# First layer's second and third modulation thirds: computed beside the attention with stationary weights, not beside the input projection

## The chip, the cores and the metric

The kernel runs as one program on one core of one Trainium2 chip. A core has a matmul engine (TensorE, PE in the rows; its loads of stationary operands are PEld), a vector engine (DVE), a scalar engine (ACT), a general engine (GpSimd, POOL) and a sync engine (SP) that issues the DMAs; each takes its instructions in the order in which they are written into the program, and they wait for one another by semaphores. The metric is the device time of one execution, in microseconds (us), lower is better.

## The reference, cut to what matters

Two layers of a transformer-like block over 256 context tokens and 1024 latent tokens, 1024 features, all in float32. Each layer draws six modulation vectors of 1024 features, for the latent tokens from `c` and for the context tokens from `c_ctx`:

```python
mod_x = (jax.nn.silu(c) @ ada_w[l] + ada_b[l])[:, None, :]          # 1024 x 6144 weights
mod_c = (jax.nn.silu(c_ctx) @ ada_w[l] + ada_b[l])[None, None, :]
sh1x, sc1x, g1x, sh2x, sc2x, g2x = jnp.split(mod_x, 6, axis=-1)     # the same for mod_c
hx = modulate(rmsnorm(xx, norm_mix_g[l]), sh1x, sc1x)               # first third: sh1, sc1
px = hx @ w_in[l]                          # columns of three mixers: GLA, attention, RWKV
mix_x = concatenate([oa_x, ob_x, oc_x]) @ w_out[l]
xx = xx + g1x * mix_x                                               # second third: g1, sh2
hx = modulate(rmsnorm(xx, norm_ffn_g[l]), sh2x, sc2x)               # third third: sc2, g2
xx = xx + g2x * swiglu(hx, ffn_w_gate[l], ffn_w_up[l], ffn_w_down[l])
```

So the first third (columns 0 to 2047) is needed before the layer's input projection, the other two (columns 2048 to 6143) only from the output projection on.

## The kernel before, in words

Features lie on the 128 partitions, tokens along the free dimension in groups of 256, 512 and 512. A dense product is made of three float32r matmuls (leading by leading, leading by trailing, trailing by leading parts), with a 128x128 weight tile stationary and up to 512 tokens moving. Weights come by DMA as `w_raw` (512 KB) and are split into two parts on ACT and DVE (`weight`, `split`, L343 and L344).

One layer runs through these stages, which are told by the names of the tiles that TensorE writes:

- the columns of RWKV of the input projection (`in_rwkv`, banks `ps_in`) with what is elementwise in them: a convolution over three tokens, decays, scans; much of that is on DVE. Results go to DRAM (`d_ab` among them);
- RWKV itself (`ps_g`, `ps_y`, `ps_w`, `ps_r`, `ps_s`) beside the other columns of the input projection, whose matmuls fill the time between (`mixers`). The first `ps_g` is its start;
- the attention (`swa_mixer`): scores `ps_ss`, softmax on DVE and ACT, transposes `ps_st` (L164), values `ps_so`, and the factors `ps_rb`; ten blocks of 128 queries in the first layer, two of them context blocks that see two tiles of keys, the others up to five. The states of GLA from the right (`ps_gu`) run beside it. Transposes, `ps_rt` and `ps_rb` share three PSUM banks (tag `t`);
- the output projection (`ps_o`, `out_first`) beside the rest of GLA (`ps_ga`, `ps_go`), the norm, the feed-forward part (`ps_gu` of `w_gate` and `w_up`, `ps_d`).

The modulation vectors of the first layer are made by `ada` (L225) with the conditioning as the stationary operand: `c32` holds the two vectors in 32 columns, the weights are the moving operand, 512 columns wide (L254). Third 0 is computed at the start. Thirds 1 and 2 come from the generator `rest_ada` in `start_mixers`, which `in_rwkv` advances by two steps after every column of RWKV; each step loads four 256 KB tiles `w_ada` and makes four matmuls. A copy to SBUF, four transposes and four additions (L258 to L267) bring a third into feature-major form, `mods`. The second layer's thirds are computed in another way beside the first layer's feed-forward part and are not touched.

During the attention, `out_start` (L1286) loads the rows of RWKV for the output projection and then the first two weight tiles of it:

```python
        for o in range(2):
            yield OS2
            first.append(out_weight(l, o, wpool))
```

Its tiles `w_raw` are a ring of two in the pool `opool`. The order of instructions in the attention and in `in_rwkv` is set by a scheduler with its own estimates; in RWKV and in the output projection TensorE's order is that in which `Weave` draws from generators.

Of the kernel before, what the change touches and what calls it, by code (L numbers as in the profile page):

```python
# [10 lines left out]
F32 = mybir.dt.float32  # L11
# [11 lines left out]
# RWKV beside dense products: ns of dense products among 3400, head start of the dense ones in ns, by layer  # L23
SHARE = (1000, 1000)
LEAD = (22000, 20000)
# ns between the steps of the states from the right
GB, GB2 = 4000, 6000
# ns between the first weights of the output projection
OS2 = 5000
# columns of the input projection kept for the end of RWKV  # L30
HOLD = 1
# features of x loaded ahead, features of the output projection that are left for its second part
XA, OT = 1, 2
# features that the vector engine leaves to GpSimd: in the output, in the modulation (by layer and norm)
PO = {768: (0, 2, 3, 5, 6), 512: (1, 3, 5), 256: (0, 3, 6)}
MG = {(0, 0): (1, 3, 5, 6), (0, 1): (0, 2, 4, 6), (1, 0): (0, 2, 4, 6), (1, 1): (0, 2, 4, 6)}
# tiles of probabilities before and after the transpose
# [20 lines left out]
# column tiles of the input projection, in the order in which they are computed  # L58
# [5 lines left out]
# columns of the per-layer parameter tile  # L64
# [81 lines left out]
def block_kernel(ctx: ExitStack, tc: tile.TileContext, a):  # L146
# [3 lines left out]
    class Tensor:  # L150
        """the tensor engine with an estimate of its time, in ns"""
# [48 lines left out]
    # decay over a chunk, by direction and pair of heads  # L200
# [14 lines left out]
    def wide(pool):  # L215
        """the two vectors as columns of 32"""
        c32 = pool.tile([P, KD, 32], F32, name="c32")
        G.memset(c32, 0.0)
        G.tensor_copy(c32[:, :, 0:2], cs)
        return c32  # L220
# [4 lines left out]
    def ada(l, r, pool, pp, tag, bufs, spool, pbufs=1, c32=None):  # L225
        """a third of the modulation vectors of a layer: columns 2048 r to 2048 (r + 1)"""
        ps = pp.tile([P, 512], F32, name="ps_ada", tag=tag, bufs=pbufs)
        for j in range(8) if c32 is None else ():
            # the sums over the tiles of features first, those over the features of a tile on the tensor engine
# [44 lines left out]

    class Norm:
        """RMS norm over the features, which lie on the partitions and along k of x"""
# [5 lines left out]
        def add(self, o, g0, n):  # L282
            # apart: not of the ring, whose slots go by the order of the program
# [17 lines left out]
        def sums(self, sq, n, first, last):  # L301
            """over the partitions, of every token"""
# [4 lines left out]
        def rstd(self, g0, n):  # L307
            """1 / sqrt(mean of squares), the same on every partition, in PSUM"""
# [13 lines left out]
        def modulated(self, l, w_, g0, n, h):  # L322
            """h[:, k, 0 / 1, :] = leading and trailing part of modulate(rmsnorm(x))"""
# [17 lines left out]
    def split(dst, src):  # L341
        """the leading and the trailing part"""
        S.copy(dst[:, 0], src)  # L343
        V.tensor_tensor(dst[:, 1], src, dst[:, 0].bitcast(F32), ALU.subtract)  # L344

    def weight(pool, src, bufs=3, raws=2, cut=0):
        """a weight tile as its leading and its trailing part"""
# [7 lines left out]
    def product(ps, n, wh, k0=0, total=None):  # L355
        """ps[:, :n] = sum over pairs of a weight tile (hi, lo) and activations (hi, lo) in float32 accuracy"""
# [7 lines left out]
    def rsqrt(pool, v, name):  # L364
        """1 / sqrt(v) in place of v, a small tile: bit guess and Newton steps"""
# [26 lines left out]
    # (column of a padded tile, token, tokens)  # L392
    PIECES = [(1, 0, 256), (258, 256, 512), (770, 768, 512)]

    def in_rwkv(l, h, wpool, pool, bpool, cpool, pp, beside, first):
        """the columns of RWKV and what is elementwise in it; the results go to DRAM"""
# [17 lines left out]
        # in the last layer the tokens of the context give keys and values only  # L414
# [3 lines left out]
        def conv(*names):  # L418
            """projection and centred shift of columns; tokens at 1:257 and 258:1282"""
# [16 lines left out]
            for nm, rw in zip(names, rws):  # L436
                for _ in range(2):
                    next(beside, None)
# [10 lines left out]
        def scan_inputs(j, o, t0, n, d):  # L449
            """a, r, kappa and beta of a pair of heads and a direction"""  # L450
# [17 lines left out]
            # exp of the decays up to a token, with a one before the first (forward) or after the last (backward)  # L468
# [70 lines left out]
        for _ in beside:  # L539
            pass  # L540

    def tokens_of(aux, tmp, y, t0, n, dst):
        """the n columns of y, token-major"""
# [7 lines left out]
    def in_rest(l, h, cols, wpool, pool, own, ypool, pp, spawn):  # L551
        """the other columns, step by step"""
# [6 lines left out]
        def drain(nm, g0, n, ps):  # L559
            # not of the ring for the first columns, whose slots go by the order of the program  # L560
# [61 lines left out]
    def in_gla(l, t0, pool, own, pp, dw):  # L622
        """what is elementwise in the linear attention, for 256 tokens"""
# [38 lines left out]
    def known(at, keys):  # L662
        """for a generator in a Weave: waits for all of the keys (stage, number from 0 on)"""
# [5 lines left out]
    class Weave:  # L669
        """Traces generators in the order in which the tensor engine takes their parts. A generator yields the  # L670
        time until its next part has its operands, or a function that returns the time from which on it has
        them (None: not known yet). Of what is ready, the first in the list goes first."""
# [9 lines left out]
        def run(self, manual=True, stay=()):  # L682
            """until all jobs have ended but those of the ranks that may stay"""
            with tc.manual_schedule(engines={mybir.EngineType.PE}) if manual else nullcontext():
                while any(j[0] not in stay for j in self.jobs):
# [11 lines left out]
                    if self.share:  # L697
                        # the dense matmuls are spread so that the engine's clock stays up
# [15 lines left out]
    def column(mh, t):  # L714
        """the columns of a token tile in the tile of its group"""
# [3 lines left out]
    def mixers(ctx_, l, t_first, ins, h, wpool, dpool):  # L719
        """RWKV beside the rest of the input projection"""  # L720
# [25 lines left out]
    def gla_states(d, t, kt, vt, St, gD, ps_of, into, n=2):  # L746
        """the states (head and key, value) behind the first n chunks of a tile, St the one before them"""
# [538 lines left out]
    def out_start(l, t_first, mh, wpool, groups, first, sums, after):  # L1286
        """what the output projection needs first, beside the attention"""
        for i, (g0, n) in enumerate(groups):
# [5 lines left out]
            for k in range(2):  # L1294
                split(mh[g0][:, 6 + k], raw[:, k, :n])
# [322 lines left out]
```

## Time and profile before

| | us |
|---|---|
| median of 3 runs | 3877.22 (3876.11 to 3885.97) |
| profiled execution, span from first to last instruction | 3864.4 |
| median less span | 12.8 |
| RWKV columns, first layer: first `ps_in` to first `ps_g` | 47.7 to 319.0 |
| RWKV beside the other columns, first layer | 319.0 to about 783 |
| attention, first layer: first `ps_ss` to first `ps_o` | 783.3 to 995.2 |
| RWKV columns, second layer | 2131.3 to 2327.5 |

The page lists no time of the profiled execution but its span, so the 12.8 us stand for what lies around the span. PE is busy for 96% of the span, DVE 49%, ACT 38%, POOL 21%; the mean granted clock of TensorE is 0.974 of full speed. Busy time of PE is modelled and overlaps between pipelined matmuls. A float32 matmul (not float32r) shows as two records, each with its own load of the stationary operand.

### The profile page before, as it was taken

The numbers are of one execution on the slowest core, as the hardware profiler recorded it, in microseconds if no ns is written. First come the engines' busy times: TensorE is split into PE (matmuls) and PEld (weight loads), VectorE is DVE, ScalarE is ACT, GpSimd is POOL, SyncE is SP. The second block draws the span as 40 slices with busy tenths as digits, with TensorE's granted clock in tenths as the row PEclk, the third lists the DMA queues.
The fourth block names the chain that finished last, engine by engine and source line by source line (L and its number), as shares of the span: only waits on it lengthen the run. The fifth ranks groups of instructions, "written<-read, shape, count | busy, mean of one in ns | idle before, by whom it ended". The sixth has DMA issues, their size and how long they took to land. (4 is left out here: it accounts for less than half of the span.)

```text
span 3864.4 us, 75751 instructions
## 1 busy us (share of the span) xinstructions
PE 3708.4 (96%) x31194; PEld 2894.2 (75%) x31194; DVE 1888.0 (49%) x3773; ACT 1457.8 (38%) x3054; POOL 821.6 (21%) x1169
## 2 busy tenths in 40 slices
PE   7999899999999999999999998899999999999998
PEld 4547677767788888888887766677777778888887
DVE  4663545566554333333334783455575643433334
ACT  4333543357334323333333443543375231111113
POOL 3111222211323223323332131222112310000002
PEclk9999999989999999999999999999899999999999
DMA  5454443331311122222211244343322211111111
GB/s 206 148 176 128 119 127 106 85 107 34 117 62 55 61 68 69 69 63 67 70 61 60 80 156 122 107 133 98 89 78 85 83 33 50 40 53 44 55 44 60
DMA packets 264826, 334.96 MB, mean 87 GB/s; under 512 B 48417, under 2 KB 197025, under 8 KB 262433
## 3 DMA queue, kind: packets, MB, share of 16 engines
q1 hardware_dynamic: 264480, 330.12, 27.2%
q8 instruction: 246, 4.03, 0.4%
q14 instruction: 100, 0.81, 0.1%
HBM read 255.15 MB, written 69.64 MB: 84 GB/s over the span
## 5 line engine op out<-in xcount | busy, mean ns | idle before, releaser
L160 PE MATMUL ps_gu<-f,w_hl 128*128 128x512 f32 (+1 forms) x5280 | 1115.9, 371 | 3.8 <-ACT sg L1386 1.5
L160 PEld LDWEIGHTS ps_gu<-f,w_hl 128*128 128x128 f32 x5280 | 914.8, 188 | 184.3 <-ACT w_hl L343 5.9
L160 PE MATMUL ps_in<-h,w_hl 128*128 128x512 f32 (+1 forms) x2928 | 726.2, 385 | 3.4 <-ACT h L331 2.8
L160 PEld LDWEIGHTS ps_in<-h,w_hl 128*128 128x128 f32 x2928 | 485.6, 193 | 161.7 <-issue 86.3
L160 PE MATMUL ps_d<-gt,w_hl 128*128 128x512 f32 (+1 forms) x2688 | 577.9, 371 | 11.0 <-DVE x L1404 9.7
L160 PEld LDWEIGHTS ps_d<-gt,w_hl 128*128 128x128 f32 x2688 | 471.0, 190 | 113.5 <-DVE x L1404 14.0
L1404 DVE SCALAR_TENSOR_TENSOR x<-ps_d,mods,x 128x512 f32<-128x512 f32 (+1 forms) x448 | 306.9, 688 | 344.1 <-PE ps_d L160 343.8
L343 ACT CAST w_hl<-w_raw 128x1024 fp32r<-128x1024 f32 (+2 forms) x214 | 197.4, 942 | 534.8 <-PE ps_d L160 359.6
L242 POOL TENSOR_TENSOR acc_ada<-acc_ada,p_ada 128x256 f32<-128x256 f32 x336 | 262.3, 816 | 612.5 <-ACT p_ada L241 465.1
L344 DVE TENSOR_TENSOR w_hl<-w_raw,w_hl 128x1024 fp32r<-128x1024 f32 (+2 forms) x214 | 238.5, 1122 | 203.2 <-ACT w_hl L343 201.5
L1387 DVE TENSOR_TENSOR sg<-sg,ps_gu 128x512 f32<-128x512 f32 (+1 forms) x110 | 69.8, 635 | 460.5 <-PE ps_gu L160 449.7
L296 POOL TENSOR_TENSOR nacc<-nacc,nsq 128x512 f32<-128x512 f32 (+1 forms) x52 | 60.7, 1167 | 827.1 <-ACT nsq L295 825.0
L1386 ACT ACTIVATE sg<-ps_gu 128x512 f32<-128x512 f32 (+1 forms) x110 | 61.1, 555 | 323.4 <-PE ps_gu L160 321.5
L1388 ACT CAST gt<-sg 128x512 fp32r<-128x512 f32 (+1 forms) x110 | 63.1, 574 | 314.1 <-DVE sg L1387 314.1
L241 ACT ACTIVATE p_ada<-w_ada,cs 128x256 f32<-128x256 f32 x336 | 154.9, 503 | 32.9 <-POOL acc_ada L242 22.7
L160 PE MATMUL ps_o<-m,w_hl 128*128 128x512 f32 (+1 forms) x720 | 164.9, 378 | 0.0
L974 DVE TENSOR_REDUCE mx<-ps_ss 128x1 f32<-128x640 f32 (+2 forms) x144 | 107.6, 747 | 106.9 <-PE ps_ss L160 106.7
L160 PEld LDWEIGHTS ps_o<-m,w_hl 128*128 128x128 f32 x720 | 124.2, 189 | 32.1 <-issue 7.3
L164 PE MATMUL ps_st<-cst,pr 128*128 128x128 f32 x640 | 110.3, 299 | 11.6 <-ACT pr L976 10.3
L976 ACT ACTIVATE pr<-ps_ss,mx 128x640 f32<-128x640 f32 (+2 forms) x144 | 106.0, 737 | 28.1 <-DVE mx L975 25.4
L344 DVE TENSOR_TENSOR pT<-ps_st,pT 128x512 fp32r<-128x512 f32 (+1 forms) x168 | 108.8, 657 | 14.6 <-ACT pT L343 13.7
L343 ACT CAST pT<-ps_st 128x512 fp32r<-128x512 f32 (+1 forms) x168 | 94.4, 565 | 57.0 <-PE ps_st L164 50.1
(289 smaller groups left out, 4793.9 us busy)
## 6 DMA issues: line engine op xcount, KB each, us to landing
w_ada<-in_ada_w_dram SPq DMA_DIRECT2D x192, 256.0 KB, 2.8
w_raw<-in_w_in_dram SPq DMA_DIRECT2D x44, 512.0 KB, 3.8
w_raw<-in_w_gate_dram SPq DMA_DIRECT2D x44, 512.0 KB, 3.6
w_raw<-in_w_down_dram SPq DMA_DIRECT2D x44, 512.0 KB, 3.7
w_raw<-in_w_up_dram SPq DMA_DIRECT2D x44, 512.0 KB, 3.6
AK<-d_ab SPq DMA_DIRECT2D x80, 256.0 KB, 3.2
d_ab<-W SPq DMA_DIRECT2D x16, 1024.0 KB, 4.1
rope<-in_rope_dram SPq DMA_DIRECT2D x20, 512.0 KB, 4.1
```

The costliest lines, as they stand in the source:

```text
L160: return nc.tensor.matmul(out, lhsT, rhs, **kw)
L164: return nc.tensor.transpose(*args)
L241: S.mul(p, w[:, k % 2], cs[:, k, s:s + 1])
L242: G.tensor_tensor(acc[:, s], acc[:, s], p, ALU.add)
L343: S.copy(dst[:, 0], src)
L344: V.tensor_tensor(dst[:, 1], src, dst[:, 0].bitcast(F32), ALU.subtract)
L974: V.tensor_reduce(m_, psf[:, :nk * P], AX.X, ALU.max)
L976: S.activation(pr[:, :nk, :].rearrange("p a n -> p (a n)"), psf[:, :nk * P], AF.Exp, bias=m_, accum_out=mx[:, 1, head:head + 1])
L1386: S.activation(sg[:, :n], pg[:, :n], AF.Silu)
L1387: V.tensor_tensor(sg[:, :n], sg[:, :n], pu[:, :n], ALU.mult)
L1388: S.copy(gt[:, 0, g0:g0 + n], sg[:, :n])
L1404: V.scalar_tensor_tensor(x[:, o, g0:g0 + n], ps[:, :n], mods[:, l, s, 40 + o:41 + o], x[:, o, g0:g0 + n], ALU.mult, ALU.add)
```

## The change

`rest_ada` and its advances in `in_rwkv` go. A new generator `ada_late` runs with the lowest rank in the Weave of the first layer's attention. It takes the 4096 columns of thirds 1 and 2 in 32 groups of 128. For a group it loads 512 KB of weights (from a copy of `ada_w` laid out so that a partition's part is contiguous), and makes eight float32 matmuls that have a 128x128 tile of weights stationary and the two conditioning vectors (2 columns) moving; one small DVE instruction adds the bias and writes `mods`. The eight matmuls of a group are called a pack below; there are 32 packs. The loads are issued one group ahead into the same ring of two `w_raw` tiles that `out_start` uses, the results take a bank of tag `t`. `out_start` now waits for the last pack before it loads its two weight tiles.

```diff
+    def ada_late(l, pool, pp, at):
+        def load(o):
+            w = pool.tile([P, KD, P], F32, name="w_raw", bufs=2)
+            SY.dma_start(w, a["ada_t"][l, o - 16])
+            return w
+        ahead = load(16)
+        yield 4000
+        for o in range(16, 48):
+            w = ahead
+            if o + 1 < 48:
+                ahead = load(o + 1)
+            ps = pp.tile([P, 512], F32, name="ps_ad", tag="t", bufs=3)[:, 0:2]
+            for k in range(KD):
+                TE.matmul(ps, w[:, k, :], cs[:, k, :], start=(k == 0), stop=(k == KD - 1))
+                yield 0
+            V.tensor_scalar(mods[:, l, :, o], ps, par[:, l, PC["adab"] + o:PC["adab"] + o + 1], None, ALU.add)
+            yield 1500
+        V.scalar_tensor_tensor(Am[:, l, 1], mods[:, l, :, 32:32 + KD], 1.0,
...
+        at["ada", 0] = TE.t
...
             for nm, rw in zip(names, rws):
-                for _ in range(2):
-                    next(beside, None)
...
                     tokens_of(aux, tmp, y[:, o:o + n], t0, n, d_v[:, :, j * P:(j + 1) * P])
-        for _ in beside:
-            pass
...
                 split(mh[g0][:, 6 + k], raw[:, k, :n])
+        if l == 0:
+            yield after(("ada", 0))
         for o in range(2):
             yield OS2
...
-        def rest_ada(bpool):
-            if l == 0:
-                c32 = wide(bpool)
-                for r in (1, 2):
-                    yield from ada(0, r, bpool, pp, "d", 3, dpool, 2, c32)
...
                 w.spawn(out_start(l, t_first, mh, opool, groups, first, *waits), 9)
+                if l == 0:
+                    w.spawn(ada_late(l, opool, pp, waits[2]), 10)
...
+    out["ada_t"] = A(f["ada_w"][0:1, :, 2 * D:].reshape(1, KD, P, 32, P).transpose(0, 3, 2, 1, 4))
```

How the instructions move, at three places. TensorE in the RWKV columns of the first layer, from the end of the first two columns on (`h_303`, `h_349` and `h_399` are the inputs of the three token groups), before:

```order
L160 MATMUL ps_in<-h_399,w_hl 128x512 x48
L160 MATMUL ps_ada<-w_ada,c_645 32x512 x3
L160 MATMUL ps_in<-h_303,w_hl 128x256 x2
L160 MATMUL ps_in<-h_349,w_hl 128x512 x2
L160 MATMUL ps_in<-h_303,w_hl 128x256 x22
L160 MATMUL ps_in<-h_349,w_hl 128x512 x8
L160 MATMUL ps_ada<-w_ada,c_645 32x512
L160 MATMUL ps_in<-h_349,w_hl 128x512 x5
L160 MATMUL ps_ada<-w_ada,c_645 32x512
```

The same place with the change:

```order
L160 MATMUL ps_in<-h_399,w_hl 128x512 x48
L160 MATMUL ps_in<-h_303,w_hl 128x256 x2
L160 MATMUL ps_in<-h_349,w_hl 128x512 x2
L160 MATMUL ps_in<-h_303,w_hl 128x256 x22
L160 MATMUL ps_in<-h_349,w_hl 128x512 x22
L160 MATMUL ps_in<-h_399,w_hl 128x512 x24
```

The 64 `ps_ada` matmuls between those of the projection are gone. At the end of this stage, the dense matmuls that stood between the last `ps_gt` and the first `ps_g` now stand earlier. TensorE at the end of the first layer's attention, before (`m_...` are the inputs of the output projection by token group):

```order
L160 MATMUL ps_rb<-rt,cst 64x128 x8
L160 MATMUL ps_so<-pT,sv 64x512
L160 MATMUL ps_so<-pT,sv 128x512
...
L160 MATMUL ps_o<-m_9562,w_hl 128x256 x18
L160 MATMUL ps_o<-m_9563,w_hl 128x512 x18
L160 MATMUL ps_o<-m_9564,w_hl 128x512 x11
```

And with the change, from the last two packs that stand inside the attention on:

```order
L164 MATMUL ps_st<-cst,pr 128x128 x4
L160 MATMUL ps_ad<-cs,w_raw 128x2 x8
L164 MATMUL ps_st<-cst,pr 128x128 x4
L160 MATMUL ps_ad<-cs,w_raw 128x2 x8
L164 MATMUL ps_rt<-cst,mx 8x128
...
L160 MATMUL ps_rb<-rt,cst 64x128 x8
L160 MATMUL ps_ad<-cs,w_raw 128x2 x64
L160 MATMUL ps_o<-m_9342,w_hl 128x256 x18
L160 MATMUL ps_o<-m_9343,w_hl 128x512 x18
```

Of the 32 packs, 24 stand among the instructions of the attention (11 before the factors `ps_rb` of the fourth block, then about two a block) and the last 8 in one piece behind it, ahead of the first `ps_o`. SP's queue at that place, before (the two loads of `w_out` stand in the middle of the attention, ahead of the queries of later blocks):

```order
L923 DMA ql<-d_q_93 128x4x128
L1281 DMA w_raw<-in_w_out_dram 128x1024
L1293 DMA w_raw<-d_mix_80 128x2x512
L769 DMA b_kt<-d_gk 128x128
L771 DMA b_vt<-d_gv 128x256
L1281 DMA w_raw<-in_w_out_dram 128x1024
```

And with the change, from the queries of the last block on:

```order
L942 DMA ql<-d_q_93 128x4x128
L279 DMA w_raw<-in_ada_t_dram 128x1024 x6
L186 DMA c_mgr<-in_cst_dram 128x256
...
L279 DMA w_raw<-in_ada_t_dram 128x1024
L1330 DMA x<-in_xT_dram 128x1280 x2
L822 DMA g_kt<-d_gk 128x128
L822 DMA g_vt<-d_gv 128x256
L279 DMA w_raw<-in_ada_t_dram 128x1024
L822 DMA g_qk<-d_g 128x4x128
L822 DMA g_vt<-d_gv 128x256
L822 DMA g_gg<-d_gg 128x2x128 x3
L279 DMA w_raw<-in_ada_t_dram 128x1024 x4
L1300 DMA w_raw<-in_w_out_dram 128x1024 x4
```

The first weights of the output projection now stand behind the last of the 32 loads, and the loads of the residual `x` and of GLA stand among the last six of them.

## Rows read from the trace of the kernel before

**Rows 1.** The page: span, and each engine's busy time, share, instructions.

```profile
span 3864.4 us, 75751 instructions
PE 3708.4 (96%) x31194; PEld 2894.2 (75%) x31194; DVE 1888.0 (49%) x3773; ACT 1457.8 (38%) x3054; POOL 821.6 (21%) x1169
```

**Rows 2.** Busy time by stretch, RWKV columns of either layer; columns in first row.

```profile
core 0: us, PE busy (x) PEld busy (x) DVE busy (x) ACT busy (x) POOL busy (x), PEclk, DMA share, GB/s
47.70:319.00 271.30, 265.96 (x1032) 155.25 (x1032) 159.86 (x206) 100.16 (x169) 57.46 (x92) 0.98 0.46 154
2131.00:2327.00 196.00, 184.48 (x791) 132.76 (x789) 146.86 (x177) 91.33 (x154) 50.44 (x90) 0.97 0.34 122
2200.00:2300.00 100.00, 100.00 (x423) 68.79 (x422) 88.94 (x107) 48.96 (x86) 29.04 (x43) 1.00 0.32 119
```

**Rows 3.** The same view of `ps_ada` alone: PE, PEld and DVE.

```profile
60.00:300.00 240.00, 61.65 (x128) 8.14 (x128) 1.37 (x2) 0.99 0.44 149
```

**Rows 4.** Timeline of PE: start, us, engine, line, operation, shapes, count, idle before.

```profile
100.61 1.04 PE L160 MATMUL ps_ada<-w_ada,c 128*32 128x512 f32 x2
101.59 2.13 PE L160 MATMUL ps_in<-h,w_hl 128*128 128x512 f32 x12
```

**Rows 5.** Timeline of PE: start and end of the RWKV columns, both layers.

```profile
47.72 0.80 PE L160 MATMUL ps_in<-h,w_hl 128*128 128x256 f32 x2 [2.75 <-ACT h L331]
...
300.64 18.45 PE L160 MATMUL ps_in<-h,w_hl 128*128 128x512 f32 x90
319.01 1.09 PE L160 MATMUL ps_g<-AK 64*64 64x128 f32 x16
...
2131.31 0.86 PE L160 MATMUL ps_in<-h,w_hl 128*128 128x512 f32 x3
...
2327.51 1.97 PE L160 MATMUL ps_g<-AK 64*64 64x128 f32 x16 [5.41 <-DMA AK<-d_ab]
```

**Rows 6.** Busy time by stretch, the attention: first layer, then start of second.

```profile
783.00:870.00 87.00, 79.93 (x515) 57.29 (x516) 56.78 (x141) 54.50 (x139) 11.85 (x19) 0.78 0.31 92
803.00:823.00 20.00, 18.07 (x117) 11.91 (x117) 13.18 (x38) 11.64 (x35) 2.81 (x5) 0.70 0.36 103
843.00:870.00 27.00, 24.35 (x169) 19.62 (x168) 18.83 (x36) 16.20 (x35) 3.21 (x4) 0.81 0.21 56
870.00:960.00 90.00, 87.08 (x631) 69.66 (x630) 61.15 (x121) 67.69 (x143) 13.58 (x18) 1.00 0.13 36
960.00:995.00 35.00, 31.00 (x180) 22.53 (x179) 20.05 (x42) 21.59 (x50) 4.21 (x8) 0.91 0.11 31
...
2783.00:2803.00 20.00, 16.04 (x76) 11.54 (x76) 11.01 (x22) 8.02 (x20) 3.24 (x4) 0.61 0.24 70
```

**Rows 7.** Float32 matmuls with 128x128 stationary, one column moving: timeline; a clock.

```profile
3853.15 2.06 PE L160 MATMUL ps_st<-cst,nsq 128*128 128x1 f32 x16
...
3843.40 0.97 PEld L160 LDWEIGHTS ps_st<-cst,nacc 128*128 128x128 f32 x4
3844.25 2.68 PEld L160 LDWEIGHTS ps_d<-gt,w_hl 128*128 128x128 f32 x12
...
3843.00:3845.00 2.00, 2.00 (x11) 2.00 (x11) 1.18 (x4) 1.03 (x4) 0.00 (x0) 0.50 0.98 357
```

**Rows 8.** DMA issues (KB each, us to landing); timeline of a `w_out` split.

```profile
w_raw<-in_w_out_dram SPq DMA_DIRECT2D x16, 512.0 KB, 3.9
x<-in_xT_dram SPq DMA_DIRECT2D x8, 640.0 KB, 5.2
...
1007.07 0.83 ACT L343 CAST w_hl<-w_raw 128x768 fp32r<-128x768 f32 x1
1008.77 0.95 DVE L344 TENSOR_TENSOR w_hl<-w_raw,w_hl 128x768 fp32r<-128x768 f32 x1
```

**Rows 9.** Timeline of PE: end of the first layer's attention.

```profile
992.11 3.25 PE L160 MATMUL ps_so<-pT,sv 128*64 128x512 f32 x7
995.15 9.15 PE L160 MATMUL ps_o<-m,w_hl 128*128 128x256 f32 x47
```

More of the change, by code (lines that the diff above doesn't have):

```diff
@@ L273, in ada @@
         yield
+    def ada_late(l, pool, pp, at):
[16 more added lines that the diff above has]
+        V.scalar_tensor_tensor(Am[:, l, 1], mods[:, l, :, 32:32 + KD], 1.0,
+                               par[:, l, PC["nffn"]:PC["nffn"] + KD].unsqueeze(1).to_broadcast([P, 2, KD]),
+                               ALU.add, ALU.mult)
+        at["ada", 0] = TE.t
     class Norm:
@@ L393, in block_kernel, with in_rwkv @@
     PIECES = [(1, 0, 256), (258, 256, 512), (770, 768, 512)]
-    def in_rwkv(l, h, wpool, pool, bpool, cpool, pp, beside, first):
+    def in_rwkv(l, h, wpool, pool, bpool, cpool, pp, first):
         lo = bpool.tile([P, 256], F32, name="lora")
@@ L1049, in swa_mixer @@
         spawn(soft(), 6)
-        return mxs, after
+        return mxs, after, at
     def rwkv_mixer(l, t_first, pool, fpool, pp, spawn):
@@ L1284, in out_weight, with out_start @@
         return raw, hl
-    def out_start(l, t_first, mh, wpool, groups, first, sums, after):
+    def out_start(l, t_first, mh, wpool, groups, first, sums, after, at):
         for i, (g0, n) in enumerate(groups):
@@ L1424, in start_mixers @@
     def start_mixers(l, t_first, e1, h, wpool, dpool, pools, first=None):
-        pp = psum_of(f"sg{l}")[0]
+        psum_of(f"sg{l}")
         cpool, px, ex = pools
-        def rest_ada(bpool):
-            if l == 0:
-                c32 = wide(bpool)
-                for r in (1, 2):
-                    yield from ada(0, r, bpool, pp, "d", 3, dpool, 2, c32)
         with ex, pool_of("inb", side="right") as bpool:
-            in_rwkv(l, h, wpool, dpool, bpool, cpool, px, rest_ada(bpool), first)
+            in_rwkv(l, h, wpool, dpool, bpool, cpool, px, first)
         return l, t_first, e1.pop_all(), h, wpool, dpool
```

## The prediction

> **What bounds the kernel now.** I read the page's engine table first: PE is busy for 3708.4 of 3864.4 us, DVE for 49% [rows 1]. Over the whole program a matmul that disappears is time that disappears, and a matmul added is time added, unless the stage in question has idle PE time or another engine close behind. So I went on to busy times by stretch, for the two stages that the change touches. In the RWKV columns of the first layer PE is busy for 265.96 of 271.30 us at a clock of 0.98 [rows 2]: PE bounds that stage. In the attention it is different. From 783 to 870 us PE is busy for 79.93 of 87 us, but the granted clock is 0.78; from 870 to 960 it is 87.08 of 90 at 1.00, and from 960 to 995 it is 31.00 of 35 at 0.91 [rows 6]. PE idles there for 14 of 212 us, and much of its busy time is slow. Last I read the timelines, for the price of single matmuls and for how each stage begins and ends [rows 4, 5, 7, 9], and the DMA table [rows 8].
>
> The page gives a span of 3864.4 us and no other time of this execution; the median of the runs is 3877.22, so 12.8 us lie around the span. My sum is made on the span, and 12.8 is added at its end.
>
> **Step 1, the input projection loses its 64 modulation matmuls.** One of them takes from 100.61 to 101.59 us, 0.98 us with its successor right behind it [rows 4]; as two records each, the 128 records of 60 to 300 us add up to 61.65 us of busy time [rows 3]. 64 x 0.98 = 62.7. That is PE's part. What is late next? DVE: it has 159.86 us of work in this stretch. The second layer's stage is the same one without modulation: it takes 196.2 us, from 2131.31 to 2327.51 [rows 5], with DVE at 146.86 us, 0.75 of it, though in its middle DVE runs at 88.94 of 100 beside a PE without a gap [rows 2]. At a share of 0.75, DVE's 159.86 us take 213 us, against 271.3 now: 58 less. By PE it is 63 less, or 66 with the small transposes gone too. At the stage's end the 90 dense matmuls of 18.45 us that stood ahead of the first `ps_g` stand earlier now, as the order shows; in the second layer PE waits 5.41 us there for AK, read back from DRAM [rows 5]. Such a wait and its neighbours could take 8 us of the 58, which gives the lower bound. I take -61, range -50 to -66. The modulation's DMAs leave this stage too, but they bounded nothing at a share of 0.46 [rows 2].
>
> **Step 2, the price of a pack.** A pack is eight float32 matmuls, each two records with a load of 128x128 each. The nearest row is the sixteen records with one moving column at the end: 2.06 us with the last one's drain, which a successor would overlap [rows 7]. At the lower clock, 0.50, four such loads take 3843.40 to 3844.25, 0.2125 each, so sixteen take 3.4 us, and 1.7 at twice the clock [rows 7]. I take 1.8 us at full clock and 3.4 at half. All 32 packs at full clock are 58 us: the work that goes from one place comes back almost whole at another, and only the idle time there is a gain.
>
> **Step 3, the attention takes 24 packs.** I count its PE work as if all at full clock. From 783 to 870: 79.93 x 0.78 = 62.3, and 11 packs x 1.8 = 19.8 make 82.1 us, which at full clock would fit into the 87 that the stretch takes now. From 870 to 995: 87.08 + 31.00 x 0.91 = 115.3, and 13 x 1.8 = 23.4 make 138.7. The question is the clock. In this trace it is low where PE does short matmuls with small pauses: at 803 to 823 PE is busy for 18.07 of 20 us, 117 records, and the clock is 0.70; at 2783 to 2803 it is 16.04 of 20 at 0.61 [rows 6]. A pack is the shortest kind of work, sixteen loads for two moving columns each, so I expect packs to lower the clock, not to hold it. For the first stretch I take 0.74, between its mean of 0.78 and the 0.70 inside it: 82.1 / 0.74 = 111, +24 us; at 0.78 it would be 105 (+18), at 0.61 135 (+48). For the second, 0.84, midway between its mean now, (90 x 1.00 + 35 x 0.91) / 125 = 0.975, and 0.70: 138.7 / 0.84 = 165, +40; at 0.975 it would be 142 (+17), at 0.78 178 (+53). The bank of tag `t` that a pack holds is one of three that the transposes and `ps_rb` also need; that works in the same direction and I put no price on it of its own.
>
> The Trainium skill ("TensorE: Matmul & The Clock Gate", section "Why this matters for your kernels") advises against idle gaps between bursts of matmuls, since an idle PE goes back to the lower clock; by that, packs in the gaps would hold the clock up. The rows at 0.70 with PE busy for 18.07 of 20 us speak against taking busy time for the measure, so this is a rival below and not my forecast.
>
> What costs nothing in the attention: the 32 small DVE additions. The two copies of `ps_ada` took 1.37 us, 0.7 each [rows 3], which bounds all 32 at 22 us; DVE is busy for 56.78 of 87 us [rows 6], and PE, with more work, hides it. The loads: 24 x 512 KB over some 270 us add 47 GB/s to 92 and 36 [rows 6], less than the 154 at which the input projection ran without a wait [rows 2]. A load waits in SP's queue until the pack two before it is done, and the queries of later blocks stand behind it; those packs stand well ahead of the blocks on PE, so I count no wait.
>
> **Step 4, the last eight packs stand alone.** Before, the first `ps_o` follows the last `ps_so` at once, 992.11 + 3.25 against 995.15 [rows 9]: nothing covers what is put between. Each load takes 3.9 us [rows 8] and the ring has two tiles, so a tile is free only when its pack is done: a pace of (3.9 + 3.4) / 2 = 3.65 us at half clock, 8 x 3.65 = 29 us; at full clock (3.9 + 1.8) / 2 = 2.85, 23 us. Two loads of `x`, 640 KB and 5.2 us each [rows 8], and GLA's stand among these loads in SP's queue and share the engines: +3. The first weight tile of the output projection was loaded long before; now its load stands behind the last pack's, and 3.9 us of load, 0.83 on ACT and 0.95 on DVE [rows 8] come to 5.7, of which 3.4 lie beside the last packs: +2. Together +34; low 23 + 4 = 27, high 40, with the first `ps_o` at half clock and the out weights waited for once more.
>
> **The sum.** -61 + 24 + 40 + 34 = +37. 3864.4 + 37 + 12.8 = 3914 us. About 0.3% (11.6 us) is what a measurement of this kernel tells from no change: faster is below 3865.6, slower above 3888.8. With every term at its low end, -66 + 18 + 17 + 27 = -4, 3873; with every term at its high end, -50 + 48 + 53 + 40 = +91, 3968.
>
> **The rivals.**
> First, packs hold the clock. In the attention they fill PE's gaps, the clock is granted at 1.00, and the two stretches take 82.1 and 138.7 us: -5 and +14; with a tail of 27, -61 - 5 + 14 + 27 = -25, 3852: faster. For it: 870 to 960 runs at 1.00 with few gaps [rows 6]. Against it: the 0.70 row. It decides from a mean clock of 0.92 on: with a tail of 34 the attention may grow by 27 to 239 us for its 220.8 us of full-clock work. Chance 0.11.
> Second, the clock stays what it was in each stretch (0.78, 0.975): -61 + 18 + 17 + 27 = +1, 3878, no change. For it: the blocks' large matmuls are all still there. Chance 0.13.
> Third, the input projection gives back less: the 18.45 us of dense matmuls covered DVE's last work and the return through DRAM, and the start of `ps_g` waits as in the second layer: -58 + 18.45 + 5.41 = -34, and the rest as forecast: +64, 3941. Against it: the second layer's stage, which has no such cover, already shows its 5.41 within 196.2 us. Chance 0.10.
> Fourth, the clock is low throughout (0.61, then 0.78): -61 + 48 + 53 + 40 = +80, 3957. For it: 0.61 in the second layer's attention; against it: full-clock stretches of 90 us. Chance 0.08.
> That the change does not do what it says is true in part: 8 of 32 packs are not beside the attention; that is step 4, not a rival.
>
> **How the numbers follow.** The forecast has 0.58, with its own range from 3890 to 3945. Faster: the first rival and a little of the second, 0.13. Same: the rest of the second and the forecast's edge, 0.14. Slower: 0.73. A range from 3862 to 3960 leaves out most of the first rival and the upper half of the fourth with some of the third, about 0.18.
>
> **What would show it.** In the profile after: the first `ps_g` near 258 us instead of 319 (step 1; right between 253 and 269, the third rival near 285). The attention from its first `ps_ss` to the last `ps_rb`, near 276 us instead of 212, with a clock well under 0.9 (step 3); 1.00 there is the first rival. Between the last `ps_rb` and the first `ps_o` some 34 us with 64 `ps_ad` matmuls that wait for `w_raw`, and a clock near 0.50 (step 4). The second layer must be as it was. Most of all, the forecast would be wrong if the clock stays up beside the packs, since with the clocks of before step 3 costs 35 us and not 64.

## The result: slower, by more than was forecast

| | before | after |
|---|---|---|
| median, us | 3876.66 (3861.83 to 3885.97, 4 runs) | 3930.57 (3925.8 to 3942.73, 4 runs) |
| ratio to before | | 1.0148, 95% interval 1.0118 to 1.0178 |
| span of the profiled execution, us | 3864.4 | 3924.3 |

The medians differ by 54 us, the spans by 59.9. The forecast was 3914, 37 us more; the measured time is 17 us above it and lies in the stated range. By stage, each read from the first and last matmul of its kind:

| first layer | before, us | after, us | difference | forecast |
|---|---|---|---|---|
| RWKV columns, first `ps_in` to first `ps_g` | 271.3 | 203.4 | -67.9 | -61 |
| RWKV beside the other columns, to the first `ps_ss` | 464.3 | 471.5 | +7.2 | 0 |
| attention, to the end of the last `ps_rb` | 208.9 | 294.6 | +85.7 | +64 |
| from there to the first `ps_o` | 3.0 | 30.5 | +27.5 | +34 |
| all that follows, second layer included | | | +7.1 | 0 |

The program's first matmul of the stage starts 0.3 us later; with it the differences add up to 59.9. Before, the last `ps_so` (3 us) stood behind the last `ps_rb`; with the change they stand ahead of it. The forecast ended the attention of before at the first `ps_o`, 211.9 us; by its bounds the attention grew by 82.7 us for the 64 that were forecast, and 30.5 us stand behind it for 34.

The page of the changed kernel, the lines that answer to [rows 1]:

```profile
span 3924.3 us, 76451 instructions
PE 3756.0 (96%) x31570; PEld 3000.8 (76%) x31570; DVE 1891.1 (48%) x3795; ACT 1454.2 (37%) x3054; POOL 823.4 (21%) x1167
```

PE has 47.6 us more busy time, though the packs replace matmuls that cost about the same at full clock. Busy time is time, not work: in this profile a pack takes 1.95 us where the clock is 1.00 and 3.54 us where it is 0.50 (747.83 and 1023.26 us in the timeline below). So the clock column has to be read beside it. Busy time by stretch of the changed kernel (columns as in [rows 2]): the RWKV columns of either layer, the attention in three parts and as a whole, the piece behind it:

```profile
48.00:251.40 203.40, 195.55 (x898) 146.10 (x898) 157.64 (x191) 98.88 (x169) 55.59 (x87) 0.98 0.33 117
2186.90:2383.00 196.10, 182.94 (x790) 132.43 (x788) 146.53 (x177) 91.14 (x154) 51.70 (x90) 0.98 0.35 123
722.90:822.00 99.10, 96.12 (x538) 74.99 (x539) 46.72 (x126) 42.05 (x112) 8.47 (x15) 0.64 0.43 118
822.00:920.00 98.00, 95.05 (x579) 80.20 (x577) 47.41 (x96) 47.82 (x103) 11.36 (x14) 0.76 0.20 59
920.00:1017.50 97.50, 97.12 (x593) 80.97 (x592) 49.37 (x105) 51.35 (x115) 9.75 (x16) 0.80 0.24 73
722.90:1017.50 294.60, 288.29 (x1707) 236.16 (x1707) 143.50 (x325) 141.22 (x330) 29.58 (x45) 0.73 0.29 84
1017.50:1048.00 30.50, 26.08 (x128) 25.71 (x128) 2.46 (x9) 1.47 (x3) 8.15 (x8) 0.53 0.64 207
```

The same view of the kernel before, the attention as a whole (its parts are [rows 6]):

```profile
783.30:992.20 208.90, 195.20 (x1316) 147.56 (x1317) 137.98 (x302) 143.48 (x330) 29.64 (x44) 0.90 0.21 59
```

Busy time times clock gives roughly the work as if at full clock: 195.20 x 0.90 = 176 us before, 288.29 x 0.73 = 210 after, 35 us more. At the clock of before, 0.90, that work would be 234 us of busy time; it was 288, so 54 us are the clock. The pauses fell from 13.7 to 6.3 us. Together: 35 / 0.90 = 39, and 54, less 7, is the 86 us by which the attention grew. The split is rough, since 35 us for 24 packs is 1.5 us each, less than the 1.95 that one takes at 1.00. None of the three parts reaches the 1.00 that the kernel before had from 870 to 960 us [rows 6].

PE's timeline (columns as in [rows 4]): a pack early in the attention, at a clock of 1.00, then the piece behind the attention, where [rows 9] had the first `ps_o` at once:

```profile
747.83 1.95 PE L160 MATMUL ps_ad<-cs,w_raw 128*128 128x2 f32 x16
...
1017.42 5.02 PE L160 MATMUL ps_ad<-cs,w_raw 128*128 128x2 f32 x32
1023.26 3.54 PE L160 MATMUL ps_ad<-cs,w_raw 128*128 128x2 f32 x16 [0.82 <-DMA w_raw<-in_ada_t_dram]
1028.42 3.55 PE L160 MATMUL ps_ad<-cs,w_raw 128*128 128x2 f32 x16 [1.61 <-DMA w_raw<-in_ada_t_dram]
1032.25 3.54 PE L160 MATMUL ps_ad<-cs,w_raw 128*128 128x2 f32 x16 [0.29 <-DVE mods L292]
1036.72 6.96 PE L160 MATMUL ps_ad<-cs,w_raw 128*128 128x2 f32 x32 [0.93 <-DMA w_raw<-in_ada_t_dram]
1044.01 3.54 PE L160 MATMUL ps_ad<-cs,w_raw 128*128 128x2 f32 x16 [0.34 <-DVE mods L292]
1048.03 0.79 PE L160 MATMUL ps_o<-m,w_hl 128*128 128x256 f32 x2 [0.48 <-ACT w_hl L367]
```

Sixteen records, a pack, take 3.54 us. Of the pauses between packs, 3.4 us are waits for the loads and 0.6 us for the DVE instruction that writes `mods`; the last wait is for the split of the first output weight.

### The profile page after: what moved, and what is told of

Its sections match the earlier page's. It is cut to its first block, busy times and chain, and to the rows that moved or that the text cites. A ratio compares the mean times of both kernels' runs of the same rounds, so it can differ in the third digit from the quotient of the medians.

```text
span 3924.3 us, 76451 instructions
## 1 busy us (share of the span) xinstructions
PE 3756.0 (96%) x31570; PEld 3000.8 (76%) x31570; DVE 1891.1 (48%) x3795; ACT 1454.2 (37%) x3054; POOL 823.4 (21%) x1167
## 5 line engine op out<-in xcount | busy, mean ns | idle before, releaser
L160 PE MATMUL ps_in<-h,w_hl 128*128 128x512 f32 (+1 forms) x2928 | 716.0, 384 | 3.4 <-ACT h L355 2.8
L242 POOL TENSOR_TENSOR acc_ada<-acc_ada,p_ada 128x256 f32<-128x256 f32 x336 | 265.1, 824 | 609.6 <-ACT p_ada L241 464.3
L164 PE MATMUL ps_st<-cst,pr 128*128 128x128 f32 x640 | 119.8, 324 | 7.4 <-ACT pr L995 7.0
```

Of the source, the lines that this page charges most:

```text
L160: return nc.tensor.matmul(out, lhsT, rhs, **kw)
L164: return nc.tensor.transpose(*args)
L242: G.tensor_tensor(acc[:, s], acc[:, s], p, ALU.add)
```

## The experiments

Each ran beside the kernel before on its chip, and ratios are to that. Stage times and clocks are from each one's profiled execution.

### Are the loads to blame, or the packs?

First experiment: the loads stay, most of the matmuls go.

```diff
-            for k in range(KD):
-                TE.matmul(ps, w[:, k, :], cs[:, k, :], start=(k == 0), stop=(k == KD - 1))
+            for k in range(1):
+                TE.matmul(ps, w[:, k, :], cs[:, k, :], start=True, stop=True)
```

> Of the eight matmuls of each pack only the first is left (the modulation vectors then lack seven eighths of their sums); the 32 loads of 512 KB, the banks, the 32 additions and the order of the waits stay. Theory A, the packs themselves (their PE work and the lower clock beside them) make the attention long: 83 of the 86 us that the attention grew by vanish, it takes about 212 us at a clock near 0.90, the piece behind it falls from 30 to some 15 us, 3832 us in all. Rival B, the loads in SP's queue and the shared banks hold the attention back: it stays over 270 us, 3900 or more.

Measured 3848.29 us, ratio 0.9952 (0.993 to 0.9974). Its attention, and one stretch near the start:

```profile
721.60:957.30 235.70, 217.35 (x1380) 167.78 (x1381) 142.78 (x335) 142.26 (x330) 30.01 (x44) 0.83 0.44 123
741.00:761.00 20.00, 19.55 (x104) 13.56 (x104) 10.19 (x36) 10.34 (x31) 3.08 (x5) 0.59 0.68 190
```

59 of the 86 us are gone, not 83, and the piece behind the attention fell to 3.0 us: theory A has most, and rival B's 270 us is wrong. But 27 us stay with almost no PE work added, at 0.59 near the start. The waits of PE in that attention (total, times, longest, us) show one that the kernel before has not:

```profile
PE ps_ad L160 <- DMA w_raw<-in_ada_t_dram: 6.5, 4, 2.6
```

Why the clock at the start is 0.59, where [rows 6] has 0.70, with one small matmul left of each pack, stays open.

Second: the opposite, the matmuls stay and the loads go.

```diff
-                ahead = load(o + 1)
...
-                TE.matmul(ps, w[:, k, :], cs[:, k, :], start=(k == 0), stop=(k == KD - 1))
+                TE.matmul(ps, eye, cs[:, k, :], start=(k == 0), stop=(k == KD - 1))
```

> The packs keep their 256 matmuls, banks and additions, but take a constant tile as the stationary operand instead of loaded weights: no load, no ring, no wait for data (the modulation vectors are then not the right ones). The run with one matmul of eight showed that the attention is still 27 us longer than in the kernel before with nearly no PE work added. Theory A1 (PE work at a low clock): the attention stays at 270 to 295 us, the piece behind it, eight packs without waits, 15 to 28 us; 3900 to 3925 us in all. Rival B (loads in SP's queue hold PE and start the low clock): those 27 us and more go, the attention takes 240 to 265 us, 3865 to 3895 us in all.

Measured 3917.8 us, ratio 1.011 (1.0085 to 1.0135). The attention and the piece behind it:

```profile
726.70:1002.50 275.80, 269.22 (x1707) 219.05 (x1707) 144.81 (x328) 143.01 (x334) 29.95 (x45) 0.79 0.16 45
1002.50:1027.80 25.30, 25.30 (x128) 25.30 (x129) 5.07 (x12) 1.64 (x4) 8.49 (x8) 0.54 0.37 129
```

The time lies in theory A1's bounds. Against the change the attention is 19 us shorter and the tail 5, but the profiled execution was the shortest of its four, 18 us under their median; by the ratios, 1.0148 against 1.011, the loads cost some 15 us in all, which is not shown, as the intervals overlap. The matmuls alone make the attention 67 us longer than before.

### What in the packs lowers the clock?

Third: the same packs, but 128 moving columns, the two vectors repeated.

```diff
-            ps = pp.tile([P, 512], F32, name="ps_ad", tag="t", bufs=3)[:, 0:2]
+            ps = pp.tile([P, 512], F32, name="ps_ad", tag="t", bufs=3)[:, 0:128]
...
-                TE.matmul(ps, w[:, k, :], cs[:, k, :], start=(k == 0), stop=(k == KD - 1))
+                TE.matmul(ps, w[:, k, :], cs[:, k, :].unsqueeze(1).to_broadcast([P, 64, 2]), ...
```

> Each pack moves its two vectors 64 times, 128 columns and not 2, by a repeating access pattern; loads, banks, waits and the number of weight loads stay. A matmul record of 512 columns took 0.49 us at full clock, so one of 128 takes about 0.12, and a pack about 1.96 us and not 1.84. Theory A1, a pack lowers the clock because almost nothing moves through the array in it: the clock of the attention rises from 0.73 to 0.95 or more, the attention takes about 225 us and not 295, 3860 us in all. Rival A2, the clock falls because of the weight loads or of pauses between short groups: it stays near 0.73, and the added work makes it 298 us, 3935 in all. Rival B (loads and banks): 3935 as well.

Measured 3883.95 us, ratio 1.0036 (1.0021 to 1.0052): by the ratios some 43 us less than the change, with more work per matmul. The attention and the piece behind it:

```profile
725.50:978.10 252.60, 245.09 (x1707) 204.09 (x1707) 141.48 (x325) 140.51 (x330) 29.32 (x45) 0.89 0.33 95
978.10:1008.20 30.10, 20.37 (x129) 19.17 (x129) 2.52 (x10) 1.55 (x3) 8.39 (x8) 0.77 0.74 232
```

The clock rose from 0.73 to 0.89, not to the 0.95 of the expectation, and the attention took 252.6 us, not 225. The work grew little, 245.09 x 0.89 = 218 for 210. Behind the attention nothing was won: PE's busy time fell to 20 us, and the loads set the 30.

Fourth to seventh: all packs inside the attention, with a higher rank and an even pace, with 2, 128 and 64 columns. The edit on the change (and the one above for the columns):

```diff
-                    w.spawn(ada_late(l, opool, pp, waits[2]), 10)
+                    w.spawn(ada_late(l, opool, pp, waits[2]), 5)
...
-            yield 1500
+            yield 3600
```

> The packs get a higher rank and a longer pace (3600 instead of 1500 between two), so that all 32 stand inside the attention, the last ahead of the factors of the last two blocks. If the tail costs what the profile shows, the 30.5 us behind the attention fall to 3, and the eight packs cost 8 x 1.84 / 0.73 = 20 us inside it: 3922 us in all. Rival: the eight packs fill pauses inside, or the attention's first blocks, now with fewer packs, keep a better clock: 3900 or less.

> Both edits, 128 moving columns and the even pace without a tail. Theory A1: as the run with 128 columns, 3884, less 27 of its tail of 30, plus eight packs of 1.96 us at a clock of 0.95, 16: 3873 us, near the kernel before. Rival A2 (weight loads lower the clock): 3895 or more.

> The same order as the runs without a tail with 2 and with 128 moving columns (345 us at a clock of 0.64, 259 us at 0.93), with 64 moving columns. By theory A1 the clock lies between the two, about 0.75, with PE work as with 2 columns: the attention takes about 300 us, 3910 us in all. Rival A2 (something else in the run with 128 columns, not the columns, held the clock): it would sit at one of the two ends.

> The run with 128 moving columns and the even pace once more, on the chip of the other two and in more rounds: 0.997 to 1.000 of the kernel before if the first measurement holds, 3866 to 3876 us.

| moving columns | median, us | ratio to before | attention, us | clock in it |
|---|---|---|---|---|
| 2 | 3945.62 | 1.0164 (1.0141 to 1.0188) | 345.2 | 0.64 |
| 64 | 3898.56 | 1.0063 (1.0038 to 1.0087) | 281.1 | 0.82 |
| 128 | 3870.07 | 0.9985 (0.997 to 1.0) | 258.9 | 0.93 |
| 128, again | 3868.15 | 0.9992 (0.9978 to 1.0006) | 265.5 | 0.90 |

The attention with 2 columns, as a whole and in two stretches of 20 us:

```profile
731.00:1076.20 345.20, 338.93 (x1828) 284.79 (x1828) 150.17 (x335) 145.11 (x330) 29.29 (x44) 0.64 0.31 85
771.00:791.00 20.00, 20.00 (x107) 16.28 (x105) 8.36 (x24) 6.92 (x19) 3.08 (x5) 0.50 0.47 125
791.00:811.00 20.00, 20.00 (x98) 16.60 (x99) 8.73 (x20) 8.46 (x20) 0.20 (x1) 0.50 0.30 88
```

And with 128:

```profile
727.50:986.40 258.90, 250.11 (x1828) 208.50 (x1828) 144.82 (x335) 140.67 (x330) 29.36 (x44) 0.93 0.39 113
767.00:787.00 20.00, 20.00 (x146) 16.05 (x145) 10.73 (x27) 10.79 (x27) 0.19 (x1) 0.83 0.60 146
787.00:807.00 20.00, 19.47 (x164) 16.41 (x162) 11.59 (x27) 10.56 (x24) 3.13 (x5) 0.91 0.50 147
```

This pair carries the verdict. The loads, the banks, the number of matmuls and the number of packs between one block's `ps_rb` and the next are the same, and the moving operand differs. With 2 columns PE is busy for every one of 40 us and the clock is 0.50, its lower level of 1.2 GHz; with 128 it is 0.83 and 0.91. Sixty-four columns lie between. (The profiled execution with 2 columns was the slowest of its five; its median lies 27 us lower, and the order of the rows stays.)

The order of instructions is not the same, although the expectation for 64 columns says so: within the blocks the scheduler interleaved packs and the attention's matmuls in another way for each width. So the order is a rival for the cause. It is out where packs stand alone, with no other matmul among them: behind the attention in the second experiment (2 columns, no loads; first line) and in the third (128 columns; second line):

```profile
1004.60:1027.80 23.20, 23.20 (x110) 23.20 (x111) 2.97 (x11) 1.43 (x3) 6.39 (x6) 0.50 0.32 109
1001.70:1008.10 6.40, 4.04 (x32) 3.72 (x32) 0.44 (x2) 0.83 (x2) 0.00 (x0) 1.00 0.62 185
```

With 2 columns the clock stays at 0.50 to the end of the piece though PE never pauses. With 128 it was at 0.50 too, from 986 to 999 us, but then rose to 1.00, with PE busy for only 4.04 of 6.40 us and the same weight loads. So neither pauses nor weight loads as such account for the low clock here; what the packs move does.

As for the tail: the expectation with 2 columns was 3922 us, or 3900 and less. Without the tail nothing was won on the change (1.0164 against 1.0148, intervals that overlap), though 27 us behind the attention are gone: the attention took them. With 128 columns the ratio fell from 1.0036 to 0.9985, some 20 us, and 3870.07 us came near the expected 3873.

### Form and place apart

Eighth: the form of the change at the old place, two packs per step beside the input projection.

```diff
-                for r in (1, 2):
-                    yield from ada(0, r, bpool, pp, "d", 3, dpool, 2, c32)
+                for o in range(16, 48):
...
+                        TE.matmul(ps, w[:, k, :], cs[:, k, :], start=(k == 0), stop=(k == KD - 1))
...
+                    if o % 2:
+                        yield
```

> The form alone: the packs of the change at the place of before, beside the input projection, two packs per step. Full-clock work of that stage is 203 + 32 x 1.84 = 262 us. Theory A1: a pack between dense matmuls of 512 columns lowers the clock less than between the attention's; clock 0.90 to 0.97 and the stage 270 to 290 us, 3875 to 3895 in all. Rival A2 (weight loads lower the clock wherever they stand): 0.80 or less, 320 us, 3925. Rival B, the clock does not matter here: 262 us, 3868.

Measured 3910.84 us, ratio 1.0113 (1.0088 to 1.0139). The projection, and the attention, now without packs:

```profile
47.50:346.70 299.20, 293.70 (x1408) 242.22 (x1408) 165.01 (x224) 101.57 (x169) 51.25 (x87) 0.83 0.41 135
818.60:1028.20 209.60, 194.87 (x1316) 146.09 (x1316) 138.25 (x302) 143.12 (x330) 29.66 (x44) 0.90 0.21 59
```

The clock of the projection falls from 0.98 [rows 2] to 0.83, and the stage takes 299 us and not 271. That is between the expectations of A1 and A2: even among dense matmuls of 512 columns, packs cost clock. The form alone costs some 42 us with no change of place, three quarters of the 54; 28 of them lie in the projection itself, and RWKV and what follows the attention account for most of the rest, as in the change.

Ninth: the place alone, the conditioning stationary and 512 weight columns moving, beside the attention.

```diff
-            ps = pp.tile([P, 512], F32, name="ps_ad", tag="t", bufs=3)[:, 0:2]
+            ps = pp.tile([P, 512], F32, name="ps_ad", tag="t", bufs=3)
...
+                    TE.matmul(ps[0:2], cs[:, k + h_, :], w[:, h_, :], start=(k + h_ == 0), stop=(k + h_ == KD - 1))
```

> The place alone: beside the attention, with the same ring, number of loads and banks, but the form of before, the two conditioning columns stationary and 512 columns of weights moving (64 matmuls of 0.98 us in eight sums, 32 small transposes). Theory A1: PE work of the attention is 167 + 40 to 63 us, but the clock stays near 0.97; the attention takes 215 to 245 us, the piece behind it some 25, 3860 to 3885 us in all, about the time of the kernel before and some 55 us below the changed one. Rival A2 and B (pauses, loads or banks): the clock stays at 0.75 and the attention takes 300 us or more, 3930 or more.

Measured 3939.14 us, ratio 1.0186 (1.0143 to 1.0229). The attention, and its longest wait:

```profile
731.40:1028.00 296.60, 273.03 (x1416) 180.59 (x1417) 145.14 (x325) 138.49 (x328) 29.18 (x44) 0.80 0.26 73
```

```profile
PE ps_ss L160 <- ACT pr L1008: 9.2, 11, 1.9
```

The same wait in the kernel before:

```profile
PE ps_ss L160 <- ACT pr L976: 4.3, 6, 1.9
```

A1's expectation failed. PE pauses for 23.6 us, and the scores wait longer for the softmax than before. The piece behind the attention grew as well, to 42.3 us for the expected 25. This kernel differs in more than the form: a sum stays in its bank of tag `t` over four loads, so for much of the time the transposes and `ps_rb` had two banks. Whether the clock of 0.80 comes from these pauses or from a stationary operand of two columns was not separated. That the work can stand beside the attention at no cost over the whole program is therefore shown only for packs with 128 columns and without a tail.

### Looking for a faster version

Tenth: TensorE relieved of nearly all of the work, the products on ACT, the sums on GpSimd, one third beside the projection and one beside RWKV.

```diff
+                        S.mul(p, w, cs[:, k, s:s + 1])
+                        G.tensor_tensor(acc[:, s], acc[:, s], p, ALU.add)
...
+                    TE.matmul(ps[:, 2 * c + s:2 * c + s + 1], acc[:, s, c * P:(c + 1) * P], ones[:, 0:1])
```

> The kernel before with neither form on TensorE: the second third's products are made on ScalarE and added on GpSimd beside the input projection, as the kernel does for the second layer (16 matmuls of 256 columns sum over the partitions), the third third in the same way beside RWKV (32 matmuls with one moving column). If TensorE's time is what counts in these stages, the first gives back 62 - 8 us of the projection, 271 to 217, and the second adds 4 to 8 us to 464 of RWKV: 3869 - 48 = 3821 us. Rival: ScalarE's 64 us in either stage delay the chain of RWKV and the projection, 3850 or more.

Measured 3949.76 us, ratio 1.0187 (1.0168 to 1.0206). The projection and RWKV, and the largest wait of each:

```profile
48.10:314.70 266.60, 218.04 (x932) 153.34 (x932) 180.69 (x199) 161.26 (x308) 156.90 (x210) 0.86 0.38 125
314.70:866.50 551.80, 474.99 (x8243) 372.51 (x8243) 249.72 (x752) 255.80 (x657) 186.96 (x297) 0.90 0.38 108
```

```profile
PE ps_bv L160 <- DVE rk L560: 23.2, 3, 20.9
```

```profile
PE ps_ad L160 <- POOL acc_ad L289: 20.1, 4, 6.8
```

The first expectation failed, and the time is 100 us above the rival's bound. PE's busy time in the projection fell to 218 us, as worked out, but it pauses for 49 us there: its longest wait, 20.9 us, is for `rk`, a DVE tile of the RWKV columns, and not for the sums. RWKV takes 88 us more. Its pauses rose from 29.5 to 76.8 us, 20.1 of them behind sums that GpSimd had not finished, and at a clock of 0.90 instead of 0.96 PE's busy time rose by 40. That ScalarE's added work is what delayed the chain of RWKV, as the rival says, is not shown.

Eleventh and twelfth: on the version with 128 columns, twelve packs early (`yield 1000 if o < 28 else 3600`), or none beside the context blocks (`yield known(at, [("p", 15)])` ahead of the first load, then a pace of 3000).

> 128 moving columns and no tail as in the run at 3870 us, but the first twelve packs at a short pace (1000), the others at 3600, so that 96 of the 256 matmuls stand ahead of the factors of the first two blocks. In the run with the first 11 packs early and 128 columns, the clock reached 1.00 between 745 and 785 us, where the even pace had 0.91 and 0.83. If the start of the attention is short of PE work that holds the clock, this brings some 5 to 10 us: 3862 us. Rival: the work only moves, 3870.

> The opposite: 128 moving columns, no tail, four packs in each of the last eight blocks, none beside the two context blocks. If the packs now hold the clock up, their absence costs at the start, where the clock was 0.74 to 0.83 in the kernel before: 3875 to 3880 us. Rival: packs lower the clock in any case, most of all where it is already low, and late ones cost less: 3860.

Measured 3874.25 us, ratio 1.0001 (0.9987 to 1.0016), for the early ones, and 3869.14, 0.9987 (0.9973 to 1.0001), for the late; attentions of 260.5 us at 0.94 and 259.3 at 0.89. Neither differs from the even pace by more than its interval. The 5 to 10 us expected from early packs did not show, and the late ones came out between their two expectations. The best versions are within 0.3% of the kernel before; none is faster beyond its interval.

## Why the prediction was right, and where its numbers were not

**Step 1** was right in its mechanism and 7 us too small: -67.9 for -61, just outside its range of -50 to -66, with the first `ps_g` at 251.4 us, ahead of the 253 that was to bound it. The wait for AK is there, 6.66 us ahead of the first `ps_g`, but PE's part was mis-sized: it counted the modulation matmuls alone, while the projection's own 776 records of `ps_in` took less time too once these were gone. Busy time of `ps_in` before and after:

```profile
47.70:319.00 271.30, 173.66 (x776) 0.98 0.46 154
48.00:251.40 203.40, 162.26 (x776) 0.98 0.33 117
```

DVE, with 157.64 us in 203.4, was not held to the share of 0.75. The third rival is out.

**Step 2**, the price of a pack, held: 3.54 us at half clock for 3.4, and 1.95 with its drain at 1.00 for 1.8. Busy time times clock gives 35 us of added work in the attention and not 24 x 1.8 = 43; it counts too little where the clock is low.

**Step 3** had the mechanism, which the pair with 2 and 128 columns shows, and mis-sized it. The clocks taken, 0.74 and 0.84, come to a mean of 0.80 over the forecast's 276 us; measured was 0.73. Its two stretches end at the factors `ps_rb` of the fourth block, by which 11 packs are done, and at the end of the attention:

```profile
722.90:847.00 124.10, 120.34 (x708) 93.92 (x708) 58.47 (x152) 56.24 (x143) 11.39 (x19) 0.68 0.40 111
847.00:1017.50 170.50, 167.95 (x1001) 142.23 (x999) 85.04 (x173) 84.98 (x188) 18.19 (x26) 0.77 0.21 64
```

The first took 124 us at 0.68, for a forecast of 111 at 0.74; the work was as counted (120.34 x 0.68 = 82 us), and the clock and 4 us of pauses, which the forecast had left out, make the 13 us. The second took 170 at 0.77, for 165 at 0.84. Its clock was missed by as much, and that it cost only 5 us is luck: busy time times clock is 129 us there, for 139 counted. The loads, counted at nothing, may have cost some 15 us with the tail's part; the runs bound that only loosely. The fourth rival, a low clock throughout, had +101 us for the attention against the 82.7 measured by the forecast's bounds: the truth lay between it and the forecast. The first rival (packs hold the clock, 1.00) and the second (0.78 and 0.975) are refuted. The Trainium skill advises against idle gaps between bursts of matmuls, since idleness brings the lower clock ("TensorE: Matmul & The Clock Gate", "Why this matters for your kernels"). The low clock of this case came without such gaps: the run with 2 columns and an even pace has 0.50 with PE busy for 20.00 of 20 us.

**Step 4** was right: 30.5 us for 34, at a clock of 0.53, with waits for `w_raw` and for the split of the first output weight. Of its parts the load pace decides, not the clock: with 128 columns PE needed 20 us instead of 26, and the piece still took 30; without loads, at a clock of 0.54, it took 25.

**Around the span** the reading was wrong, without harm to the forecast. The profiled execution of the changed kernel took 3926.04 us for a span of 3924.3, so 1.8 us lie around a span; the 12.8 between the profile of before and the median of other executions were mostly how executions differ. Either way the 3914 is the median of before with 37 us added. But the profile of before shows a short execution, some 10 us under its median, and that of the change one 4.5 under its own, so the stages above add up to more than the 54 us between the medians.

Not forecast: RWKV's 7.2 us, of which 5.4 are pauses of PE (29.5 to 34.9 us), and 7 us behind the attention. RWKV took 469 to 484 us in the runs with packs of every kind, also 471.8 in the eighth, whose projection is as long as ever, and what follows the first `ps_o` took 2870 to 2893 us in the experiments, for 2869 before. One profile of before is too few to say whether that is the change or how executions differ; it stays open. By spans these 14 us come on top of the miss in step 3, and the errors of steps 1 and 4, 7 and 3 us the other way, hid part of it: that the sum came out within 17 us of the measured median is in part luck.

## What to carry to other kernels

Count a moved matmul at the clock that it will itself bring about. A group of many weight loads with two columns each looked as cheap as what it replaced, 1.8 us for two matmuls of 0.98, but the clock of the attention around it fell from 0.90 to 0.73; read the granted clock beside busy time, and try a wider moving operand before another place. Work that is moved out of a full stage needs room for all of it in the next: here the last quarter stood behind the attention with nothing beside it.

## What the runs showed that was not expected

A matmul with more columns made the program faster: repeating the two vectors 64 times, useless work, took some 43 us off the change, and 75 us off the even pace (3945.62 to 3870.07). PE was busy without a gap and stayed at 1.2 GHz for 40 us. And taking away the tail brought nothing with 2 columns and some 20 us with 128: what a place is worth depended on the clock there.
